# A transformer layer in fp32 on one core: transfers issued one step later, one pair of PSUM pools for all stages

## The chip, the core and the metric

The kernel runs on one core of a Trainium2 chip. Its time is the device time of one execution in microseconds (us); the medians below are of three runs. The core has five engines with in-order instruction streams: TensorE (PE; its weight loads are listed as PEld), VectorE (DVE), ScalarE (ACT), GpSimd (POOL) and SyncE (SP). SP only issues transfers here; a transfer waits in SP's queue until its buffer is free, and what is behind it in the queue waits too. ScalarE's and GpSimd's own queues carry a few more transfers. Matmul results go to PSUM, which has eight banks; each accumulator of this kernel takes a bank.

## The reference

Two token groups go through one layer: 128 context tokens and 256 latent tokens, D = 2048. Cut to what matters:

```python
def trunk_layer(x, cond, lw, attend):
    sh1, sc1, g1, sh2, sc2, g2 = modulation(cond, w_mod, b_mod)     # silu(cond) @ w_mod + b_mod
    h = rms_norm(x, n1) * (1 + sc1) + sh1
    q, k, v, u = project_in(h, w_in, q_g, k_g)                      # q, k RMS-normed per head
    attn = attend(q, k, v)                  # latent: 2-D windows with bias, plus cached context keys
    x = x + g1 * token_mixing(h, attn, u, w_na_proj, w_fnet_proj, w_gate, w_o)
    h2 = rms_norm(x, n2) * (1 + sc2) + sh2
    return x + g2 * swiglu(h2, w_gate_up, w_down), k, v
# token_mixing: (sigmoid gates * (attn @ w_na_proj, fourier(u) @ w_fnet_proj)) @ w_o
```

The outputs are both groups' tokens and the context's normed keys and values.

## The kernel before, in words

All 384 tokens go through every weight matrix together. Each operand is split into a high part (rounded, by ScalarE) and a low part (the rest, by VectorE), and a product is three matmuls (`mm3`, lines 140 to 143). **Units.** The weights come as 464 units of two 128-row tiles by 512 columns (512 KB each; some of one tile). `load_unit` (L179) puts a unit's load in SP's queue, `split_unit` (L189) makes `wh` (ACT, L137) and `wl` (DVE, L138), and `next_unit` (L202) hands PE a unit that was split two calls earlier. So a `wl` that is late by more than two units makes PE wait at the first matmul that reads it.

**Side work** is written as Python generators (`Paced`, L54) that advance by steps. A `behind` generator gets a tick in every `next_unit`, after the split; a `front` generator gets three ticks in a unit: before the split, after it, and in `mid_unit` (L198), half-way through the unit's matmuls. A rate says how many steps a tick is worth. Nothing is ordered by a planner: the order of instructions on each engine is the order in which these steps are written out. `Ahead` (L78) keeps loads a fixed number of items in front of their use; `more()` issues the next one.

**Stages**, in order of time: (1) transposes and modulated norm of x; (2) `w_in` (L619 to 647): groups of k tiles, the last group of nine tiles over eight 512-column chunks in the order 6, 7, 0 to 5; a chunk of the last group takes five units, the fifth of one tile. When a chunk is done, `after(ci)` (L589) joins `behind`: it stores the chunk and, for chunks 0 to 3 (q and k), computes the per-head norms on DVE, scales k (L610) and stores new_k. (3) `w_gate` (L984 to 998): eight passes of eight units, four accumulators each; at a pass's last unit the accumulators are copied out (`gst`, L997), the first two by DVE instead of ACT when one of the last three ticks had softmax exponentials, and stored from ACT's queue (L998). In front of it run the Fourier mixing (L660) and then the attention, eight head pairs of 15 ticks each, written in `PAIR` (L44); the modulation's rows run in front at 0.5 steps a tick. (4) `w_fnet_proj` and `w_na_proj` (L1037 to 1054), then `mixed` (L1026) gates and splits the sum; (5) `w_o` (L1142 to 1170), with x2 transposed in `behind` (`transposed`, L1123); (6) the SwiGLU feed-forward (L1266 to 1332), whose first pass also runs `inverse` (L1177) and the last `transposed`.

**Modulation rows.** `mod_rows` (L279) computes four of the six modulation vectors on DVE (L309, L311) from `w_mod` tiles `wmr`, each of which is used in two steps; per half vector there are 34 steps, the last of them a four-matmul sum (L321) and the addition of a bias row (L326).

**PSUM.** In stages 1 to 4 there are two pools of four banks, `ps` (tiles `mm`) and `pa` (tiles `at`). Most stages take accumulators from a ring, `acc_tile`: four `mm`, then three `at`, and so on without a restart (L270). The stages 5 and 6 have pools of their own over the same eight banks (L1061 to 1076): four `mm8`, three `at8` and one for the modulation rows. A pool hands out the bank that has been free longest.

Of the kernel before, what the change touches and what calls it, by code (L numbers as in the profile page):

```python
# [19 lines left out]
P = 128  # L20
# [22 lines left out]
PREP = [1.3, 1.8, 2.3, 2.3]  # L43
PAIR = "qk,b,pv,s0 m0,e0 i0,,s1 m1,e1 i1,,t0,v,,t1,,"  # L44
RATES = [1.455, 0.5, 1.1, 0.937, 0.452]
# [50 lines left out]
def trunk_kernel(ctx: ExitStack, tc: tile.TileContext, io: dict):  # L96
# [163 lines left out]
    with ExitStack() as ph:  # L260
        ps = ph.enter_context(tc.tile_pool(name="ps", bufs=4, space=PSUM))
        pa = ph.enter_context(tc.tile_pool(name="pa", bufs=4, space=PSUM))

# [5 lines left out]

        ring = itertools.cycle([mm_tile] * 4 + [at_tile] * 3)  # L270

        def acc_tile():

            return next(ring)()

        md_tile = at_tile


        def mod_rows(ty):  # L279

            def load(cc, k):
                wm = rpool.tile([P, 2, CH], F32, tag="wm", bufs=3, name=nm("wmr"))
                c0 = ty * D + cc * 2 * CH
                nc.sync.dma_start(
                    wm, w_mod[k * P : (k + 1) * P, c0 : c0 + 2 * CH].rearrange("p (i n) -> p i n", i=2)
                )
                return wm

            src = Ahead(load, [(cc, k) for cc in range(2) for k in range(KT)], 3)
            yield
            for cc in range(2):
# [8 lines left out]
                for k in range(KT):  # L302
                    _, wm = src.take()
                    for cnd in range(2):
                        if cnd:
                            yield
                        sc = csz[:, k, cnd : cnd + 1]
                        if k == 0:
                            nc.vector.tensor_scalar_mul(acc[:, cnd], wm, sc)  # L309
                        else:  # L310
                            nc.vector.scalar_tensor_tensor(  # L311
                                out=acc[:, cnd], in0=wm, scalar=sc, in1=acc[:, cnd], op0=ALU.mult, op1=ALU.add
                            )
                    src.more()
                    yield
# [105 lines left out]
        with ExitStack() as pha:  # L421
# [137 lines left out]
            def rows_and_columns():  # L559
                for ty in (2, 4, 3, 5):  # L560
                    yield from mod_rows(ty)
                    if ty in (3, 4):
                        yield
                        yield from columns(ty)
                    rows_done.add(ty)
                    yield
# [22 lines left out]
            def after(ci):  # L589
                a = acc[ci]  # L590
                if not 2 <= ci < 4:
                    nc.sync.dma_start(s_qkvu[ci], a)
# [11 lines left out]
                if ci < 2:  # L604
                    yield from inv_sqrt(rq[:, :, ci * 8 : (ci + 1) * 8], ss, HD, [P, NT, 8])
                else:
                    rk = small.tile([P, NT, 8], F32, tag="rk", name=nm("rk"))
                    yield from inv_sqrt(rk, ss, HD, [P, NT, 8])
                    a4 = a.rearrange("p t (h d) -> p t h d", d=HD)
                    nc.vector.tensor_mul(a4, a4, rk.unsqueeze(3).to_broadcast([P, NT, 8, HD]))  # L610
                    nc.sync.dma_start(s_qkvu[ci], a)
                    yield
                    nk = tmp.tile([P, 8, HD], F32, tag="junk", bufs=1, name=nm("nk"))
                    nc.vector.tensor_mul(nk, a4[:, 0], kg_row.unsqueeze(1).to_broadcast([P, 8, HD]))
                    nc.sync.dma_start(
                        new_k[:, (ci - 2) * CH : (ci - 1) * CH], nk.rearrange("p h d -> p (h d)")
                    )

            for gi, (k0, n) in enumerate(GROUPS):  # L619
                prep.due, prep.rate = DUE[gi], PREP[gi]  # L620
                if gi == len(GROUPS) - 1:
                    behind.append(Paced(expand_rpb()))
                for ci in ORDER:
                    po = [(mm_tile if gi < len(GROUPS) - 1 else acc_tile)() for _ in range(NT)]
# [35 lines left out]
        def fourier():  # L660
            with ExitStack() as st:
# [73 lines left out]
                for _ in range(6):  # L735
                    yield
                uH, uL = split_table("u", u)
                u = load_u(1)
                yield
                yield  # L740
                for pair in range(2):
                    for gi in range(2):
# [6 lines left out]
                        if pair + gi < 2:  # L749
                            uH, uL = split_table("u", u)  # L750
                            if pair == 0:
                                u = load_u(gi + 2)
# [55 lines left out]
        def attention_pair(hp, wk, values_before):  # L808
# [9 lines left out]
            def turned():  # L818
# [21 lines left out]
                nc.vector.tensor_sub(kL[:, TOK:], pk[:, TOK:], fr(kH[:, TOK:]))  # L840
                qks[0].more()

# [4 lines left out]
            def scores(qt):  # L847
# [17 lines left out]
                for j in range(2):  # L865
# [10 lines left out]
                    if qt == 0:  # L876
# [3 lines left out]
                        )  # L880
                if qt:
                    biases[0].more()

            def maxima(qt):
# [43 lines left out]
            def split_v():  # L928

                v = t["v"] = wk.tile([P, 4, 4, HD], F32R, tag="v", name=nm("v"))  # L930
                vj = vp.rearrange("p k (j d) -> p k j d", j=2)
                nc.scalar.copy(v[:, :, 0::3], vj)
                nc.vector.tensor_sub(v[:, :, 1:3], vj, fr(v[:, :, 0::3]))
                vs[0].more()

# [21 lines left out]
            def before():  # L957
                if values_before:
                    values_before()

            work = {
                "qk": turned, "b": masked, "pv": before, "v": split_v,
                **{f"{n}{j}": functools.partial(f, j) for j in range(2) for n, f in (
                    ("s", scores), ("m", maxima), ("e", exps), ("i", inverses), ("t", keys_first))},
# [19 lines left out]
        for fc8 in range(8):  # L984
            po = [mm_tile() for _ in range(4)]
            for u in range(0, KT, 2):
                wH, wL = next_unit()
                for f in range(4):
# [6 lines left out]
                    if u == KT - 2:  # L995
                        st = gst.tile([P, TOK], F32, tag="st", name=nm("gst"))
                        (nc.vector.tensor_copy if f < 2 and any(soft) else nc.scalar.copy)(st, po[f][:, :TOK])  # L997
                        nc.scalar.dma_start(s_gate[fc8][:, f], st)  # L998
        br_work.drain()
# [26 lines left out]
        def mixed(f4, gl):  # L1026
            for f in range(4):
# [3 lines left out]
                split(mixH[kt], mixL[kt], gl[0][:, f])  # L1031
                if f == 3:
                    gates.more()
                    gates.more()
                yield

        for f4 in range(4):  # L1037
            gl = [None, None]
# [21 lines left out]

    ps = ctx.enter_context(tc.tile_pool(name="ps8", bufs=4, space=PSUM))  # L1061
    pa = ctx.enter_context(tc.tile_pool(name="pa8", bufs=3, space=PSUM))
    pmd = ctx.enter_context(tc.tile_pool(name="pmd8", bufs=1, space=PSUM))

    def mm_tile():
        return ps.tile([P, CH], F32, tag="mm8", name=nm("mm"))

    def at_tile():
        return pa.tile([P, CH], F32, tag="at8", name=nm("at"))

    ring = itertools.cycle([mm_tile] * 4 + [at_tile] * 3)

    def acc_tile():
        return next(ring)()

    rows_psum["tile"] = lambda: pmd.tile([P, CH], F32, tag="md8", name=nm("md"))
    x2p = ctx.enter_context(tc.tile_pool(name="x2p", bufs=1))
# [307 lines left out]
```

## Time and profile before

| | |
|---|---|
| median of 3 runs | 2057.76 us (2057.05 to 2057.89) |
| the profiled execution | 2057.49 us, of which its span is 2055.7 us |
| PE busy in the span | 2030.5 us, 99% |
| DVE, ACT, POOL busy | 1248.7, 758.1 and 43.6 us |
| DMA engines' mean share, SP's queue | 58.8% |
| moved | 390 MB, 190 GB/s |

The profiled execution's own time is its span and 1.8 us around it. PE's busy time is the union of its matmuls, whose ends are modelled. Idle time of an engine is listed in front of the instruction that ended it, with what released it.

### The profile page before, as it was taken

To read this page: it belongs to the slowest core of one execution; us is meant where nothing else is said; L and a number is where in the kernel's file an instruction comes from. 1 tells how busy PE (TensorE), PEld (TensorE's weight loads), DVE (VectorE), ACT (ScalarE), POOL (GpSimd) and SP (SyncE) were. 2 spreads that over 40 slices of the span, in tenths; PEclk is the share of its full clock that TensorE was granted. 3 is DMA by queue.
4 is the path that set the end of the run, shared out by engine and by line. 5 is a ranking of instruction groups with operands and counts; after the bars stand their busy time and mean duration, and the time that the engine had idled before them with its cause. 6 is when DMAs were issued, how large, how long until landed. Compare 5 with 4: busy or idle time off the path is not lost.

```text
span 2055.7 us, 27509 instructions
## 1 busy us (share of the span) xinstructions
PE 2030.5 (99%) x10986; PEld 1843.7 (90%) x10986; DVE 1248.7 (61%) x1528; ACT 758.1 (37%) x1135; POOL 43.6 (2%) x92
## 2 busy tenths in 40 slices
PE   7999999999999999999999999999999999999999
PEld 5657888999999999888998999899989998999897
DVE  5634899688986787775845454544454434333456
ACT  5323232456665443334533332223322232233222
POOL 1000000000001000001000000000000000000000
PEclk9999999999999999999999999999999999999999
DMA  9887878677775775754454455544555444444453
GB/s 327 299 315 219 298 257 313 209 211 236 221 219 162 258 253 188 248 182 149 119 184 150 154 157 160 158 138 150 163 158 160 125 123 133 125 132 123 134 164 123
DMA packets 220000, 390.46 MB, mean 190 GB/s; under 512 B 28080, under 2 KB 64960, under 8 KB 219872
## 3 DMA queue, kind: packets, MB, share of 16 engines
q1 hardware_dynamic: 212704, 382.13, 58.8%
q10 hardware_dynamic: 4672, 6.31, 0.9%
q8 instruction: 86, 1.41, 0.3%
q0 software_dynamic: 2496, 0.27, 0.1%
q14 instruction: 42, 0.34, 0.1%
HBM read 371.81 MB, written 20.51 MB: 191 GB/s over the span
## 4 chain that ended last, share of the span: by engine, by line
PE 94%; DVE 2%; DMA 1%; issue 1%; SPq 1%; ACT 1%; ACTq 0%; DVEq 0%
PE mm L141 20%; PE mm L143 19%; PE mm L142 19%; PE at L143 11%; PE at L141 11%; PE at L142 11%; PE at L389 1%; DMA wm<-in_w_mod 1%; DVE accr L311 1%; PE at L856 1%; PE at L924 1%; PE at L946 1%; SPq L181 0%; SPq L365 0%; DVE wl L138 0%
## 5 line engine op out<-in xcount | busy, mean ns | idle before, releaser
L138 DVE TENSOR_TENSOR wl<-wraw,wh 128x1024 fp32r<-128x1024 f32 (+1 forms) x464 | 559.2, 1206 | 674.9 <-ACT wh L137 674.0
L137 ACT CAST wh<-wraw 128x1024 fp32r<-128x1024 f32 (+1 forms) x464 | 480.7, 1037 | 1027.9 <-PE at L142 260.3
L141 PE MATMUL mm<-hH,wh 128*128 128x384 f32 x1152 | 389.6, 338 | 1.8 <-DVE gst L997 1.2
L143 PE MATMUL mm<-hH,wl 128*128 128x384 f32 x1152 | 385.5, 335 | 0.0
L142 PE MATMUL mm<-hL,wh 128*128 128x384 f32 x1152 | 385.2, 334 | 0.0
L311 DVE SCALAR_TENSOR_TENSOR accr<-wmr,csz,accr 128x1024 f32<-128x1024 f32 x240 | 304.8, 1278 | 0.1
L141 PEld LDWEIGHTS mm<-hH,wh 128*128 128x128 f32 x1152 | 216.3, 188 | 8.3 <-issue 2.6
L142 PEld LDWEIGHTS mm<-hL,wh 128*128 128x128 f32 x1152 | 216.4, 188 | 0.0
L143 PEld LDWEIGHTS mm<-hH,wl 128*128 128x128 f32 x1152 | 216.3, 188 | 0.0
L143 PE MATMUL at<-hH,wl 128*128 128x384 f32 x640 | 213.8, 334 | 0.0
L141 PE MATMUL at<-hH,wh 128*128 128x384 f32 x640 | 213.8, 334 | 0.0
L142 PE MATMUL at<-hL,wh 128*128 128x384 f32 x640 | 213.8, 334 | 0.0
L141 PE MATMUL mm<-wh,hH 128*128 128x512 f32 x422 | 168.8, 400 | 1.8 <-DVE gl L1053 1.2
L142 PE MATMUL mm<-wl,hH 128*128 128x512 f32 x422 | 165.0, 391 | 0.9 <-DVE wl L138 0.9
L143 PE MATMUL mm<-wh,hL 128*128 128x512 f32 x422 | 164.7, 390 | 0.0
L143 PE MATMUL mm<-wh,cL 128*128 128x512 f32 x352 | 137.1, 389 | 0.0
L141 PE MATMUL mm<-wh,cH 128*128 128x512 f32 x352 | 137.0, 389 | 0.0
L142 PE MATMUL mm<-wl,cH 128*128 128x512 f32 x352 | 137.0, 389 | 0.0
L141 PEld LDWEIGHTS at<-hH,wh 128*128 128x128 f32 x640 | 120.2, 188 | 0.2
L142 PEld LDWEIGHTS at<-hL,wh 128*128 128x128 f32 x640 | 120.2, 188 | 0.2
L143 PEld LDWEIGHTS at<-hH,wl 128*128 128x128 f32 x640 | 120.2, 188 | 0.0
L141 PEld LDWEIGHTS mm<-wh,hH 128*128 128x128 f32 x422 | 79.4, 188 | 33.7 <-issue 11.9
(288 smaller groups left out, 2616.2 us busy)
## 6 DMA issues: line engine op xcount, KB each, us to landing
wraw<-in_w_gate_up SPq DMA_DIRECT2D x176, 512.0 KB, 3.7
wmr<-in_w_mod SPq DMA_DIRECT2D x128, 512.0 KB, 4.2
wraw<-in_w_down SPq DMA_DIRECT2D x88, 512.0 KB, 3.7
wm<-in_w_mod SPq DMA_DIRECT2D x64, 512.0 KB, 6.9
wraw<-in_w_gate SPq DMA_DIRECT2D x64, 512.0 KB, 5.1
wraw<-in_w_in SPq DMA_DIRECT2D x56, 512.0 KB, 6.1
wraw<-in_w_o SPq DMA_DIRECT2D x32, 512.0 KB, 5.3
wraw<-in_w_fnet_proj SPq DMA_DIRECT2D x16, 512.0 KB, 6.3
```

What stands on the lines that cost most here:

```text
L137: nc.scalar.copy(H, x)
L138: nc.vector.tensor_sub(L, x, fr(H))
L141: nc.tensor.matmul(out, aH, bH, start=start, stop=False)
L142: nc.tensor.matmul(out, aH, bL, start=False, stop=False)
L143: nc.tensor.matmul(out, aL, bH, start=False, stop=stop)
L311: nc.vector.scalar_tensor_tensor(out=acc[:, cnd], in0=wm, scalar=sc, in1=acc[:, cnd], op0=ALU.mult, op1=ALU.add)
L389: nc.tensor.matmul(pm[q : q + 32, :w], csz[:, k, :], wm[:, ty, kk + par, :], start=k < 2, stop=k >= KT - 2, tile_position=(0, q), skip_gro ...
L856: nc.tensor.matmul(po[j][:, cols], qx[rows[j], q], kx[rows[j], k], start=i == 0, stop=i == 2, tile_position=(j * HD, 0),)
L924: nc.tensor.transpose(o[:, i * P : (i + 1) * P], sc[:, j, c0 : c0 + P], ident)
L946: nc.tensor.matmul(po[j][:, CTX:TOK].rearrange("p (t q) -> p t q", t=2), w[1 + kc], x.rearrange("p (t b) q -> p t b q", t=2)[:, :, 2 * kc ...
```

## The change

It has five parts. (a) The `w_mod` row tiles of all four vectors have one `Ahead`, and the next load is issued between the two uses of a tile, when the tile before is done with, not after the second use. (b) `after` gets an empty step before its stores, and each store of a normed chunk is issued a step after the DVE instruction that makes its data. (c) In the Fourier mixing, `load_u` is issued a step after the split that frees its buffer; in the attention the three `more()` calls become ticks of their own (`lq`, `lb`, `lv`) in empty places of `PAIR`; in `mixed` the gate loads come a step later. (d) The four stores of a gate pass are issued after all four copies. (e) `ps` and `pa` live through all stages, the modulation rows take `at` tiles to the end, and the ring is three `at`, then four `mm`; it is restarted at the last `w_in` group and ahead of stage 4.

```diff
-PAIR = "qk,b,pv,s0 m0,e0 i0,,s1 m1,e1 i1,,t0,v,,t1,,"
+PAIR = "qk,b,pv,s0 m0,e0 i0,lq,s1 m1,e1 i1,,t0 lb,v,,t1,lv,"
...
-        ps = ph.enter_context(tc.tile_pool(name="ps", bufs=4, space=PSUM))
-        pa = ph.enter_context(tc.tile_pool(name="pa", bufs=4, space=PSUM))
+        ps = ctx.enter_context(tc.tile_pool(name="ps", bufs=4, space=PSUM))
+        pa = ctx.enter_context(tc.tile_pool(name="pa", bufs=4, space=PSUM))
...
-        ring = itertools.cycle([mm_tile] * 4 + [at_tile] * 3)
+        ring = None
+
+        def new_ring():
+
+            nonlocal ring
+            ring = itertools.cycle([at_tile] * 3 + [mm_tile] * 4)
...
+            return Ahead(load, [(ty, cc, k) for ty in ROWS for cc in range(2) for k in range(KT)], 3)
-            src = Ahead(load, [(cc, k) for cc in range(2) for k in range(KT)], 3)
-            yield
...
                     for cnd in range(2):
                         if cnd:
+                            if ty != ROWS[0] or cc + k:
+                                src.more()
                             yield
...
-                    src.more()
                     yield
...
             def rows_and_columns():
-                for ty in (2, 4, 3, 5):
-                    yield from mod_rows(ty)
+                src = row_weights()
+                yield
+                for ty in ROWS:
+                    yield from mod_rows(ty, src)
...
             def after(ci):
                 a = acc[ci]
+                yield
                 if not 2 <= ci < 4:
                     nc.sync.dma_start(s_qkvu[ci], a)
...
                     nc.vector.tensor_mul(a4, a4, rk.unsqueeze(3).to_broadcast([P, NT, 8, HD]))
+                    yield
                     nc.sync.dma_start(s_qkvu[ci], a)
-                    yield
                     nk = tmp.tile([P, 8, HD], F32, tag="junk", bufs=1, name=nm("nk"))
                     nc.vector.tensor_mul(nk, a4[:, 0], kg_row.unsqueeze(1).to_broadcast([P, 8, HD]))
+                    yield
                     nc.sync.dma_start(
...
                 if gi == len(GROUPS) - 1:
                     behind.append(Paced(expand_rpb()))
+                    new_ring()
...
                 uH, uL = split_table("u", u)
+                yield
                 u = load_u(1)
                 yield
-                yield
                 for pair in range(2):
...
                         if pair + gi < 2:
                             uH, uL = split_table("u", u)
+                            yield
                             if pair == 0:
                                 u = load_u(gi + 2)
                         yield
...
-                qks[0].more()
...
-                if qt:
-                    biases[0].more()
...
-                vs[0].more()
...
+                **{n: lambda of=of: of[0].more() for n, of in (("lq", qks), ("lb", biases), ("lv", vs))},
...
-                        nc.scalar.dma_start(s_gate[fc8][:, f], st)
+                        sts.append(st)
+            for f, st in enumerate(sts):
+                nc.scalar.dma_start(s_gate[fc8][:, f], st)
...
                 if f == 3:
+                    yield
                     gates.more()
                     gates.more()
                 yield
 
+        new_ring()
         for f4 in range(4):
...
-    ps = ctx.enter_context(tc.tile_pool(name="ps8", bufs=4, space=PSUM))
-    pa = ctx.enter_context(tc.tile_pool(name="pa8", bufs=3, space=PSUM))
-    pmd = ctx.enter_context(tc.tile_pool(name="pmd8", bufs=1, space=PSUM))
...
-    ring = itertools.cycle([mm_tile] * 4 + [at_tile] * 3)
...
-    rows_psum["tile"] = lambda: pmd.tile([P, CH], F32, tag="md8", name=nm("md"))
```

## Rows read from the trace of the kernel before

**Rows 1.** The page's first part: busy us of each engine, share of the span, instructions.

```profile
PE 2030.5 (99%) x10986; PEld 1843.7 (90%) x10986; DVE 1248.7 (61%) x1528; ACT 758.1 (37%) x1135; POOL 43.6 (2%) x92
```

**Rows 2.** Busy time by stretch: the stretch and its length in us, then us busy (instructions) of PE, PEld, DVE, ACT and POOL, the granted share of TensorE's clock, the DMA engines' share and GB/s.

```profile
0.00:30.00 30.00, 16.47 (x136) 12.08 (x137) 15.34 (x40) 14.75 (x36) 6.03 (x16) 0.85 0.98 295
300.00:345.00 45.00, 43.51 (x197) 36.13 (x196) 44.66 (x49) 13.16 (x14) 0.00 (x0) 1.00 0.87 302
1340.00:1700.00 360.00, 360.00 (x1956) 341.99 (x1955) 167.80 (x167) 104.53 (x118) 6.29 (x13) 1.00 0.48 145
```

**Rows 3.** What PE's matmuls waited for, over the span: us in total, times, longest us.

```profile
PE mm L141 <- DVE gl L1053: 1.2, 1, 1.2
PE mm L141 <- DVE gst L997: 1.2, 1, 1.2
...
PE mm L142 <- DVE wl L138: 0.9, 2, 0.5
PE at L143 <- DVE uL L138: 0.8, 1, 0.8
PE mm L141 <- DVE acc L645: 0.6, 1, 0.6
...
PE at L1129 <- DVE xL L1135: 0.5, 1, 0.5
```

**Rows 4.** What SP's queue waited for: the two largest lines.

```profile
SPq L181 <- DVE wl L138: 997.5, 315, 9.0
SPq L286 <- DVE accr L311: 391.8, 101, 12.0
```

**Rows 5.** DMA issues of the moved loads: out<-in, queue, count, KB each, median us from issue to landing.

```profile
wmr<-in_w_mod SPq DMA_DIRECT2D x128, 512.0 KB, 4.2
...
gl<-s_gate SPq DMA_DIRECT2D x8, 768.0 KB, 6.1
...
kp<-s_qkvu SPq DMA_DIRECT2D x8, 192.0 KB, 6.1
```

**Rows 6.** Timeline of PE at the end of `w_in`: start us, duration us, engine, line, operation, shapes, count, and in brackets the idle us ahead of it with its releaser. The first two lines are the first matmuls of the last chunk's first and second units.

```profile
318.36 0.39 PE L141 MATMUL mm<-wh,hH 128*128 128x512 f32 x1
...
322.44 0.39 PE L141 MATMUL mm<-wh,hH 128*128 128x512 f32 x1
323.37 0.50 PE L142 MATMUL mm<-wl,hH 128*128 128x512 f32 x1 [0.54 <-DVE wl L138]
```

**Rows 7.** Timelines of DVE and, last line, ACT near the end of `w_in`, same columns.

```profile
295.21 1.23 DVE L138 TENSOR_TENSOR wl<-wraw,wh 128x1024 fp32r<-128x1024 f32 x1 [1.41 <-ACT wh L137]
...
297.55 0.30 DVE L159 RECIPROCAL rss<-rss 128x24 f32<-128x24 f32 x1
...
298.53 1.76 DVE L610 TENSOR_TENSOR acc<-acc,rk 128x1536 f32<-128x1536 f32 x1
300.21 1.22 DVE L138 TENSOR_TENSOR wl<-wraw,wh 128x1024 fp32r<-128x1024 f32 x1
...
326.82 1.22 DVE L138 TENSOR_TENSOR wl<-wraw,wh 128x1024 fp32r<-128x1024 f32 x1
...
298.20 1.06 ACT L137 CAST wh<-wraw 128x1024 fp32r<-128x1024 f32 x1 [3.03 <-PE at L143]
```

**Rows 8.** Timelines of DVE and PE where the Fourier mixing waits, same columns.

```profile
382.18 0.95 DVE L138 TENSOR_TENSOR uL<-fraw,uH 128x768 fp32r<-128x768 f32 x1
...
383.19 0.39 PE L143 MATMUL at<-latH,uL 128*128 128x258 f32 x1 [0.78 <-DVE uL L138]
```

**Rows 9.** Timelines of DVE, ScalarE's queue (ACTq) and PE around the end of the seventh gate pass, same columns.

```profile
641.49 0.18 DVE L906 RECIPROCAL sm<-sm 128x4 f32<-128x4 f32 x1 [0.73 <-ACT sc L898]
641.89 0.69 DVE L326 TENSOR_TENSOR row<-row,at 128x512 f32<-128x512 f32 x1 [0.22 <-issue]
642.50 1.01 DVE L997 COPY gst<-mm 128x384 f32<-128x384 f32 x2
...
644.44 0.33 ACTq L998 DMA_DIRECT2D s_gate<-gst  x1
...
643.10 0.44 PE L141 MATMUL mm<-hH,wh 128*128 128x384 f32 x1 [1.20 <-DVE gst L997]
```

**Rows 10.** Timelines of PE and DVE in a gate unit in which a head pair's second exponentials run and no pass ends (unit 41 of 0 to 63), same columns: the last tick's transposes ahead of the next unit, and DVE's end of the unit.

```profile
563.25 1.04 PE L924 MATMUL at<-ident,sc 128*128 128x128 f32 x8
...
563.99 0.17 DVE L906 RECIPROCAL sm<-sm 128x2 f32<-128x2 f32 x1 [0.16 <-ACT sc L898]
564.07 1.26 DVE L311 SCALAR_TENSOR_TENSOR accr<-wmr,csz,accr 128x1024 f32<-128x1024 f32 x1
```

**Rows 11.** Timelines of PE, ACT and DVE at the start of `w_o`, same columns.

```profile
816.07 0.47 PE L141 MATMUL mm<-wh,hH 128*128 128x512 f32 x1 [1.21 <-DVE gl L1053]
...
822.80 1.23 DVE L138 TENSOR_TENSOR wl<-wraw,wh 128x1024 fp32r<-128x1024 f32 x1 [0.40 <-ACT wh L137]
```

**Rows 12.** Timelines of PE and ACT in the feed-forward's third unit, same columns.

```profile
962.26 0.49 PE L1188 MATMUL mm<-ident,r 128*128 128x128 f32 x3
962.80 0.52 PE L1129 MATMUL mm<-ident,x 128*128 128x128 f32 x3
...
962.28 1.05 ACT L137 CAST wh<-wraw 128x1024 fp32r<-128x1024 f32 x1 [0.91 <-PE mm L142]
963.23 0.47 ACT L1189 COPY rB<-mm 128x384 f32<-128x384 f32 x1
```

More of the change, by code (lines that the diff above doesn't have):

```diff
@@ L268, in at_tile, with row_weights, load @@
             return pa.tile([P, CH], F32, tag="at", name=nm("at"))
-        ring = itertools.cycle([mm_tile] * 4 + [at_tile] * 3)
+        ring = None
+        def new_ring():
+            nonlocal ring
+            ring = itertools.cycle([at_tile] * 3 + [mm_tile] * 4)
         def acc_tile():
             return next(ring)()
+        new_ring()
         md_tile = at_tile
-        def mod_rows(ty):
-            def load(cc, k):
+        ROWS = (2, 4, 3, 5)
+        def row_weights():
+            def load(ty, cc, k):
                 wm = rpool.tile([P, 2, CH], F32, tag="wm", bufs=3, name=nm("wmr"))
@@ L289, in load, with mod_rows @@
                 return wm
-            src = Ahead(load, [(cc, k) for cc in range(2) for k in range(KT)], 3)
-            yield
+            return Ahead(load, [(ty, cc, k) for ty in ROWS for cc in range(2) for k in range(KT)], 3)
+        def mod_rows(ty, src):
             for cc in range(2):
@@ L985, in trunk_kernel @@
             po = [mm_tile() for _ in range(4)]
+            sts = []
             for u in range(0, KT, 2):
@@ L1035, in mixed @@
                 yield
+        new_ring()
         for f4 in range(4):
@@ L1058, in trunk_kernel @@
         behind[:] = [rows]
-    ps = ctx.enter_context(tc.tile_pool(name="ps8", bufs=4, space=PSUM))
-    pa = ctx.enter_context(tc.tile_pool(name="pa8", bufs=3, space=PSUM))
-    pmd = ctx.enter_context(tc.tile_pool(name="pmd8", bufs=1, space=PSUM))
[L1065 to L1069, printed above, removed]
-    ring = itertools.cycle([mm_tile] * 4 + [at_tile] * 3)
-    def acc_tile():
-        return next(ring)()
-    rows_psum["tile"] = lambda: pmd.tile([P, CH], F32, tag="md8", name=nm("md"))
     x2p = ctx.enter_context(tc.tile_pool(name="x2p", bufs=1))
```

## The prediction

> **What bounds the kernel now.** I read the page's shares first, then the stretches, then PE's waits, then the timelines around each wait. TensorE is busy for 2030.5 of 2055.7 us [rows 1], so only 25.2 us of the span are open to any reordering. The stretches say where: 13.5 of them lie in the first 30 us, and from 1340 to 1700 us PE has none [rows 2]. The start is bound by transfers (the DMA engines are 98% busy there [rows 2]), and the change leaves its loads, their order and the matmuls alone; the transposes only take their banks in another order. I cost the start at nothing. The granted clock is 1.00 in the later stretches [rows 2], so no wait there has cost clock.
>
> What is left are single waits [rows 3]: at the end of `w_in` for two late `wl` (0.9) and for an accumulator's bank (0.6); in the Fourier mixing for `uL` (0.8); at a gate pass's end for the copy `gst` (1.2); at the start of `w_o` for a bank that `gl` still reads (1.2); and 0.5 in the x2 transposes. None of them is a wait for a weight or a stored tensor. SP's queue does wait a lot, 997.5 us for `wl` and 391.8 us for the row sums [rows 4], but the 4-deep `wraw` covers that: no line of PE's waits names `wraw`. So the first half of the change's title can move PE only through the steps that it inserts, which shift DVE's work; the second half can move it through banks. A measurement of this kernel can tell about 0.2%, 4.1 us, from no change.
>
> **The change part by part.**
>
> *Row loads.* A load now has three steps from issue to use where it had four. At 1.455 steps a unit and 4.08 us a unit (322.44 less 318.36 [rows 6]) that is 8.4 us; a tile lands in 4.2 us [rows 5]. Later stages step more slowly per us. Cost 0; without that cover DVE would stand in its queue and the next `wl` behind it. SP no longer holds the weights behind a DVE addition, worth 0 for the reason above. One loader for four vectors drops one step at each change of vector, so the second vector runs one step earlier than now and the third two.
>
> The page "DMA: Bandwidth & Descriptors" of the Trainium skill, section "Rules for kernel authors", says to issue a transfer early and wait for it late, which speaks against every such delay here. By it the sum would be larger wherever a load's cover ends; the rows show twice the landing time as cover, so I add nothing.
>
> *Other moved loads.* `lq` goes five ticks later; ten ticks, over three units and 12 us, remain before its use, against 6.1 us [rows 5]; `lb` and `lv` move by three ticks with seven and twelve left. The gate loads come half a unit later with three units left, against 6.1 us [rows 5]. Cost 0 each.
>
> *Gate stores.* Their issues used to stand between ScalarE's copies, one of them behind a DVE copy. Now four come in a row after the copies. ScalarE is 37% busy [rows 1] and casts two units ahead. Cost 0, with a rival below.
>
> *Steps in `after`.* For a k chunk the norm and scale (L159 to L610) move from the fourth unit of the next chunk to its fifth, the half unit, and the new_k product from the fifth to the next chunk's first. DVE is full here, 44.66 of 45 us [rows 2]. Now the scale of chunk 2 fills the time from 297.55 until the cast at 298.20 ends at 299.26 [rows 7]; then DVE would be idle there for 1.7 us, and the scale, 2.66 us (297.55 to 300.21), comes behind that `wl`. Today 26.6 us lie between the `wl` at 300.21 and the one at 326.82 [rows 7]. Counted from 299.3, with 2.7 more for chunk 2's scale and 0.6 less for chunk 3's new_k product, the latter starts at about 328.0 and ends at 329.2. It is read by the last chunk's third unit, which with no wait before it begins at 318.36 + 2 x 4.08 = 326.52 [rows 6], and 0.23 later reads `wl`: a wait of some 2.2 us where 0.9 stand now. Bounds are 0.9 and 2.2. I take 1.6, half-way, because the count leans on ScalarE's square root falling where I put it, and the trace does not show it there.
>
> *Banks at the end of `w_in`.* The restarted ring gives the last group's eight chunks 24 accumulators, 24 = 3 x 7 + 3, so the last chunk has three `at`, and the gate stage's four `mm` are free: the 0.6 goes. Bounds 0 and 0.6; I take all of it.
>
> *Fourier and attention ticks.* `uL` is split in the tick after the weights' split and read at the next tick, half a unit later; `uL` ends 0.8 us too late [rows 8]. With the added tick PE reads it half a unit (2 us) later still: the 0.8 goes. The branch adds three such ticks, exactly one unit, so every head pair runs one unit later against the gate passes. A pair's exponentials run in units 20 + 5p and 21 + 5p now, 21 + 5p and 22 + 5p after. Passes end with units 7, 15, ... 55, 63. Now the first exponentials meet an end at 55 (the 1.2 wait) and the second at 31. After, the first meet 31, the second meet 47, and 55 meets neither.
> At 55 the copy stands behind a reciprocal, which waits for ScalarE's exponentials, and behind the bias row's 0.69 us [rows 9]; the wait of 1.2 goes. At 31 that row is not in front of the copy, since the rows' steps are one earlier, and their four-matmul sum reaches PE ahead of the boundary: bounds 0 and 0.5; I take 0.
> At 47 a row accumulation is in front of the copy. Unit 41 shows that pattern without a boundary: reciprocal at 563.99, accumulation from 564.07, so the copy (half of 1.01 us [rows 9]) would end at 565.8, and 0.1 later PE could start; its transposes end at 564.29 [rows 10]. New wait 1.6, bounds 0.4 (no accumulation there) and 1.6. I take 1.6, since the rows step on the same ticks as before.
>
> *Start of `w_o`.* Without a restart `w_o` begins with three `mm` that stage 4 freed a set earlier, so the 1.2 goes and PE starts at 816.07 - 1.21 = 814.86 [rows 11]. DVE still has the drained `mixed` in front of the `wl` that ends at 824.03 [rows 11]; the third unit, from 814.86 + 8.17, reads it at 823.26. So 0.7 comes back; bounds 0 and 1.2.
>
> *First feed-forward pass.* Ring position 44 = 6 x 7 + 2 gives `at` and three `mm`, where now two `mm` are left. `inverse` and the last `transposed` then share one bank: the transposes at 962.80 must wait for the copy `rB`, which stands behind a cast and ends at 963.70 [rows 12]. New wait 1.0 (0.1 to restart), bounds 0 and 1.1. The x2 transposes keep their single free bank, and their 0.5.
>
> *Sum.* Gone: 0.9 + 0.6 + 0.8 + 1.2 + 1.2 = 4.7. New: 1.6 + 1.6 + 0.7 + 1.0 = 4.9. On the profiled execution's 2057.5 that makes **2057.7 us**; the median shown is 0.3 above that execution, well inside what can be told. Upper bounds of the new waits (2.2 + 0.5 + 1.6 + 1.2 + 1.1 = 6.6) give 2059.4, lower bounds (0.9 + 0 + 0.4 + 0 + 0 = 1.3) 2054.1.
>
> **The rivals.**
>
> *The waits go and nothing comes back.* Then 2057.5 - 4.7 = 2052.8. For it: five of the waits stand where a bank or a step order is changed. Against it: DVE is 99% busy in one of those places and the new order queues the same work there. The Trainium skill's page "Perfetto Trace Analysis", section "Optimizing Tensor Performance", says that independent matmul groups should rotate through different banks so that one's evacuation overlaps the next group. By that rule this rival is the outcome; the rows agree for the banks (1.8 of the 4.7), and for the rest they name late DVE work instead. Chance 0.12.
>
> *ScalarE falls behind at the gate passes.* The four stores in a row (three more issues after the last copy than now) hold the next cast, `wl` waits behind it, and PE pays at each pass. At 0.33 us an issue [rows 9] that is 1.0 us, eight times: 2057.7 + 8.0 = 2065.7. It decides only if the delay exceeds what two units' lead, 8 us, leaves over; ScalarE's share speaks against it. Chance 0.06.
>
> *The banks don't come as the ring says.* A pool hands out banks by their release, so the two bank waits (0.6 and 1.2) may stay; then the 0.7 of `w_o` and perhaps the 1.0 of the feed-forward don't come either. 2057.7 + 1.8 - 0.7 = 2058.8, or 2057.8. Chance 0.17. The forecast itself has 0.65.
>
> **How the numbers follow.** Likeliest 2057.7, its own range 2055.6 to 2059.6. The range of 8 in 10, 2054.1 to 2060.4, takes in all lower bounds and a further new wait of about a microsecond above the upper ones; it leaves out the first two rivals (0.18). Faster by over 0.2% (below 2053.65) is most of the first rival, 0.10; slower by over 0.2% (above 2061.9) is the second and a little for what I have not seen, 0.07; the rest, 0.83, is no change.
>
> **What would show it.** Right: PE's waits lose `gl`, `uL` and the `acc` line at 341 us; a wait for `gst` stands near the end of gate unit 47 (some 596 us) and none at 643; a wait of 1 us for `rB` near 963; SP's wait for the row sums shrinks from 391.8 us while the time stays. Wrong: a PE total under 2026 us, any PE wait of a kind not named here over 2 us, or casts that wait for `wraw`.

## The result and the profile after

The changed kernel takes 2062.48 us (median of 14 runs, 2060.44 to 2064.16) where the kernel before takes 2057.93 (14 runs beside it): a ratio of 1.002, 95% interval 1.0013 to 1.0027, so it is slower by some 4.5 us. The forecast was 2057.7 with a range up to 2060.4. The profiled execution took 2062.87 us, of which its span is 2061.1.

The page's shares, to be read beside [rows 1]: PE's busy time rose as well, by 2.8 us, though it computes the same.

```profile
PE 2033.3 (99%) x10986; PEld 1845.8 (90%) x10986; DVE 1248.5 (61%) x1528; ACT 758.2 (37%) x1135; POOL 44.0 (2%) x92
```

PE's waits after (us in total, times, longest), beside [rows 3]. The waits for `gl`, for `uL`, and for the accumulator at 341 us are gone, as forecast; the 1.8 for `wl` ends `w_in`, the 0.8 is `w_o`'s, and 0.6 and 0.4 are the feed-forward's. New are two waits for `gst`: 2.7 behind DVE where 1.6 was forecast, and 1.6 behind ACT, which was not foreseen.

```profile
PE mm L141 <- DVE gst L1011: 2.7, 1, 2.7
...
PE at L142 <- DVE wl L138: 1.8, 1, 1.8
PE mm L141 <- ACT gst L1011: 1.6, 1, 1.6
...
PE mm L142 <- DVE wl L138: 0.8, 1, 0.8
PE mm L1131 <- ACT rB L1191: 0.6, 1, 0.6
...
PE mm L1190 <- DVE vL L1137: 0.4, 1, 0.4
```

SP's waits after, beside [rows 4]. The first half of the change's title did what it says: SP stands 81.9 us for the row additions where it stood 391.8, and waits for the weights' own four buffers instead (`wl`, 1340.8 where it was 997.5). None of it reaches PE.

```profile
SPq L181 <- DVE wl L138: 1340.8, 405, 9.4
SPq L293 <- DVE accr L323: 81.9, 51, 4.9
```

Where the two new waits stand, in the timeline of PE after (start, length, instruction, idle time before it and what ended it): the end of gate unit 23 and the end of gate unit 47. In both the pass's last matmuls and a group of transposes are done, and the next pass's first matmul wants a bank that a copy `gst` still reads. The last line is the group of transposes that follows the second wait.

```profile
462.26 0.82 PE L937 MATMUL at<-ident,sc 128*128 128x128 f32 x6
464.63 0.45 PE L141 MATMUL mm<-hH,wh 128*128 128x384 f32 x1 [1.55 <-ACT gst L1011]
...
596.16 1.04 PE L937 MATMUL at<-ident,sc 128*128 128x128 f32 x8
599.86 0.45 PE L141 MATMUL mm<-hH,wh 128*128 128x384 f32 x1 [2.66 <-DVE gst L1011]
...
605.71 0.82 PE L937 MATMUL at<-ident,sc 128*128 128x128 f32 x6
```

Three stretches around the second wait (busy time of each engine with its instructions, then the granted clock, DMA share and GB/s). PE was busy for 1.44 of 3.4 us up to 601.30; then the clock was granted at half, 1.2 GHz instead of 2.4, for 3.4 us, and PE started 13 matmuls where it started 23 in the 3.4 us that follow. This lengthens PE's busy time by some 1.6 us, since the same matmuls take longer; the rest of the 2.8 belongs to this one execution (the second profile below has the same half clock, and PE is busy for 2030.2 us in it). In the stretches of the kernel before, such as the later ones of [rows 2], the clock is full once the start is over.

```profile
597.90:601.30 3.40, 1.44 (x8) 1.45 (x9) 2.28 (x4) 1.92 (x5) 0.00 (x0) 1.00 0.92 288
601.30:604.70 3.40, 3.40 (x13) 3.40 (x12) 2.01 (x3) 2.54 (x4) 0.00 (x0) 0.50 0.95 293
604.70:608.10 3.40, 3.40 (x23) 3.37 (x22) 3.40 (x5) 1.76 (x3) 0.00 (x0) 1.00 0.78 191
```

The account, in PE's idle time after less before: end of `w_in` 1.75 - 1.49, `uL` -0.78, unit 23 +1.55, unit 47 +2.66, the old `gst` wait at 643 us -1.20, `w_o` 0.76 - 1.21, feed-forward +0.95. That is 3.0. The 3.4 us at half speed cost 1.6 us (experiment 6), which makes 4.6, against 4.55 between the medians. Between the two profiled executions it is 5.4, since PE's first `w_in` matmul came 0.8 us later as well (30.49 against 29.68); the second profile below shows that this is no part of the change.

### The profile page after: what moved, and what is told of

Read it like the earlier page. It is cut to its first block, busy times and chain, and to the rows that moved or that the text cites. A ratio compares the mean times of both kernels' runs of the same rounds, so it can differ in the third digit from the quotient of the medians.

```text
span 2061.1 us, 27504 instructions
## 1 busy us (share of the span) xinstructions
PE 2033.3 (99%) x10986; PEld 1845.8 (90%) x10986; DVE 1248.5 (61%) x1528; ACT 758.2 (37%) x1135; POOL 44.0 (2%) x92
## 4 chain that ended last, share of the span: by engine, by line
PE 92%; DVE 3%; ACT 2%; DMA 2%; issue 1%; SPq 1%; ACTq 0%; DVEq 0%
PE mm L141 19%; PE mm L142 18%; PE mm L143 18%; PE at L142 11%; PE at L143 11%; PE at L141 11%; PE at L400 1%; DMA wm<-in_w_mod 1%; DVE accr L323 1%; DVE wl L138 1%; PE at L958 0%; PE at L872 0%; ACT wh L137 0%; PE at L937 0%; PE at L332 0%
## 5 line engine op out<-in xcount | busy, mean ns | idle before, releaser
L141 PE MATMUL mm<-hH,wh 128*128 128x384 f32 x1232 | 416.8, 338 | 4.2 <-DVE gst L1011 2.7
L143 PE MATMUL mm<-hH,wl 128*128 128x384 f32 x1232 | 412.9, 335 | 0.0
L142 PE MATMUL mm<-hL,wh 128*128 128x384 f32 x1232 | 412.6, 335 | 0.0
L141 PEld LDWEIGHTS mm<-hH,wh 128*128 128x128 f32 x1232 | 231.9, 188 | 10.4 <-issue 4.0
L142 PEld LDWEIGHTS mm<-hL,wh 128*128 128x128 f32 x1232 | 231.9, 188 | 0.0
L143 PE MATMUL at<-hH,wl 128*128 128x384 f32 x560 | 187.1, 334 | 0.0
L141 PE MATMUL at<-hH,wh 128*128 128x384 f32 x560 | 187.1, 334 | 0.0
L142 PE MATMUL at<-hL,wh 128*128 128x384 f32 x560 | 187.1, 334 | 0.0
L143 PE MATMUL mm<-wh,cL 128*128 128x512 f32 x312 | 121.6, 390 | 0.0
L142 PE MATMUL mm<-wl,cH 128*128 128x512 f32 x312 | 121.5, 389 | 0.0
```

The costliest lines, as they stand in the source:

```text
L141: nc.tensor.matmul(out, aH, bH, start=start, stop=False)
L142: nc.tensor.matmul(out, aH, bL, start=False, stop=False)
L143: nc.tensor.matmul(out, aL, bH, start=False, stop=stop)
```

## The experiments

The first theory was that the three Fourier ticks cost the time: they run every head pair one unit later against the gate passes. The rivals were the loads with their added steps, and the banks. Ratios are to the kernel before on the same chip, with 95% intervals; each variant has 11 runs.

**1. The ticks taken back out of the phase.** The changed kernel, its Fourier branch begun three ticks earlier.

```diff
-                for _ in range(6):
+                for _ in range(3):
                     yield
```

> After, with the Fourier branch begun three ticks (one unit) earlier, so that the attention stands against the gate passes as before; loads, stores, added steps and PSUM pools stay as after. Theory (the shift of one unit costs the time: the waits for gst at 464 us, 1.8, and at 600 us, 2.9, and the half clock behind the latter, 1.6): these three go, the wait of 1.2 at 643 us returns, so 2062.5 - 6.3 + 1.2 = 2057.4. Rival (loads and added steps, seen in the start's 0.95, cost the time): 2062.5 within 0.5, the gst waits merely elsewhere.

2058.7 us, ratio 1.0000 (0.9992 to 1.0009). Both new waits are gone and the clock is full. PE's waits for `gst` in this kernel come to two short ones, at 510 and 643 us:

```profile
PE mm L141 <- DVE gst L1011: 0.4, 2, 0.3
```

The phase carries the loss. The wait at 643 came back as 0.28, not as 1.2. The expected sum was 0.5 below the kernel before; the interval is 1.7 below to 1.9 above.

**2. The ticks alone**, in the kernel before.

```diff
+                yield
                 u = load_u(1)
                 yield
-                yield
...
                             uH, uL = split_table("u", u)
+                            yield
                             if pair == 0:
```

> Before, with the three Fourier ticks alone. Theory: 2057.9 - 0.9 (uL) - 1.3 (gst at 643) + 1.8 + 2.9 + 1.6 = 2062.0, with gst waits near 464 and 600 us and a stretch of half clock behind the second. Rival (loads and added steps): what the prediction said of these ticks, 2057.9 - 0.9 - 1.3 + 1.6 = 2057.3, and the clock stays at full speed.

2061.53 us, ratio 1.0016 (1.0007 to 1.0025). The total is the theory's, but not by its terms: the clock stayed full, the wait at unit 47's end is 1.58 and not 2.66, and there is one of 1.07 at the end of unit 31 (510.58). These three, less the waits that went (0.78 and 1.20), make 2.2 of the 3.3 measured; the rest is inside the interval. PE's timeline at the three pass ends:

```profile
463.42 0.45 PE L141 MATMUL mm<-hH,wh 128*128 128x384 f32 x1 [1.54 <-ACT gst L998]
...
510.58 0.45 PE L141 MATMUL mm<-hH,wh 128*128 128x384 f32 x1 [1.07 <-DVE gst L998]
...
599.15 0.45 PE L141 MATMUL mm<-hH,wh 128*128 128x384 f32 x1 [1.58 <-DVE gst L998]
```

So the forecast's 1.6 for unit 47 is what the ticks alone do, and another part of the change adds 1.1 and the half clock.

**3. The pools alone**, in the kernel before.

```diff
-        ps = ph.enter_context(tc.tile_pool(name="ps", bufs=4, space=PSUM))
+        ps = ctx.enter_context(tc.tile_pool(name="ps", bufs=4, space=PSUM))
...
+            ring = itertools.cycle([at_tile] * 3 + [mm_tile] * 4)
...
+        new_ring()
         for f4 in range(4):
...
-    ps = ctx.enter_context(tc.tile_pool(name="ps8", bufs=4, space=PSUM))
```

> Before, with the one pair of PSUM pools and the restarted rings alone. Both theories: the bank wait of 0.6 at 341 us and 1.2 at 816 us go, 0.7 for wl comes at 828, 1.0 near 966 us for vL and rB: 2057.9 - 0.1 = 2057.8. If the banks explain the slow start (transposes in another order), PE's first matmuls of w_mod columns come 0.8 us later and the time is 2058.7.

2057.65 us, ratio 0.9998 (0.9989 to 1.0007): as forecast. The 341 and 816 us waits are gone, `w_o` has 0.76 for `wl`, the feed-forward 0.38 and 0.57. The first `w_in` matmul stands at 29.59 (29.68 before), so the banks don't make the start later.

**4. The moved loads and stores alone**, with the steps in `after`, without the Fourier ticks and the pools.

```diff
+            return Ahead(load, [(ty, cc, k) for ty in ROWS for cc in range(2) for k in range(KT)], 3)
...
             def after(ci):
                 a = acc[ci]
+                yield
...
-                        nc.scalar.dma_start(s_gate[fc8][:, f], st)
+                        sts.append(st)
+            for f, st in enumerate(sts):
+                nc.scalar.dma_start(s_gate[fc8][:, f], st)
```

> Before, with all moved loads and stores and the steps added for them (row loads, after, gate stores, lq lb lv, gates), without the Fourier ticks and without the PSUM part. Theory: only the end of w_in gets longer, by 0.9: 2058.8, and 643 keeps its wait of 1.2. Rival (loads and added steps cost the time): 2061 to 2062.5, with the start 0.8 to 0.95 later and more waits for wl.

2059.99 us, ratio 1.001 (1.0001 to 1.0019), between the two expectations. PE's waits that differ from before:

```profile
PE mm L142 <- DVE wl L138: 1.8, 1, 1.8
...
PE mm L141 <- DVE acc L654: 1.2, 1, 1.2
...
PE mm L141 <- DVE gst L1003: 0.6, 1, 0.6
```

The end of `w_in` costs 1.8 where it cost 0.9, and the bank wait behind it 1.2 where it cost 0.6, since DVE is late for both; the pools take that second one away in the full change. The wait at 643, which was expected to stay at 1.2, halved. These make 0.8 of the 1.7 measured; the rest is inside the interval, and no wait shows it.

**5. The changed kernel again**, with no line of it edited, for a second profile.

> The changed kernel once more, for a second profile. If the stretch of half clock behind the wait of 2.66 us at 600 is of the kernel, it is there again near 601 to 605 and the time is 2062 to 2063; if it was of that one execution, the clock stays at full speed there and the profiled execution is some 1.6 us shorter, 2061. If the start's 0.8 was of that execution, the first w_in matmul stands between 29.6 and 30.3 us, not at 30.49.

2061.95 us, ratio 1.0021 (1.0013 to 1.003). The wait (2.72) and the half clock are there again, 596.90 to 600.30; the first `w_in` matmul stands at 29.50, before the 29.68 of the kernel before. The start varies between executions; the half clock is the kernel's. This execution took 2059.98 us, 2.9 less than the first: 1.0 of it lies before that matmul, and 1.8 between 79 and 179 us, where the same 500 matmuls took 100.20 us in the first profile and 98.43 here, both at full clock. PE's waits behind that stretch agree within 0.06 us between the two profiles. So one execution's time can't tell a microsecond here, but its waits can.

```profile
593.50:596.90 3.40, 0.84 (x8) 0.60 (x6) 3.24 (x5) 3.08 (x9) 0.00 (x0) 1.00 0.98 298
596.90:600.30 3.40, 3.25 (x10) 3.25 (x11) 1.26 (x4) 1.66 (x4) 0.00 (x0) 0.50 1.06 279
```

**6. The row addition of unit 47 half a unit later**, in the changed kernel; the later steps of the rows come one tick later with it.

```diff
+                if fc8 == 5 and u == KT - 2:
+                    rows.due -= 0.5
                 wH, wL = next_unit()
```

> After, with the bias row's addition of gate unit 47 put half a unit later, behind DVE's two gst copies. Theory (the wait at 600 us is this addition, 1.26, on top of DVE's lag): 2.66 becomes 1.4; and if the half clock hangs on that long wait, it goes too: 2062.5 - 1.3 - 1.6 = 2059.6. Rival (the exponentials' chain alone sets the copy): 2.66 stays within 0.2 and the time is 2062.5. If the clock falls whatever the wait: 2061.2.

2059.47 us, ratio 1.0009 (1.0000 to 1.0018). DVE now copies right behind the reciprocal, PE waits 1.58, and the clock stays at 2.4 GHz. Against experiment 5, on the same chip, 2.5 us are gone, 1.1 of them wait; the other 1.4 is left for the half clock. The traces give its price more closely: the next transposes start 5.85 us behind the wait's end in the first profile (605.71 less 599.86) and 4.28 behind it here (601.07 less 596.79), so 1.57.

```profile
596.12 0.17 DVE L919 RECIPROCAL sm<-sm 128x2 f32<-128x2 f32 x1 [0.16 <-ACT sc L911]
596.20 1.00 DVE L1013 COPY gst<-mm 128x384 f32<-128x384 f32 x2
...
596.79 0.44 PE L141 MATMUL mm<-hH,wh 128*128 128x384 f32 x1 [1.58 <-DVE gst L1013]
...
601.07 0.82 PE L937 MATMUL at<-ident,sc 128*128 128x128 f32 x6
```

**7. The table for the exponentials loaded earlier**, in the changed kernel.

```diff
                 values = None
+                warm = small.tile([P, 1], F32, tag="warm", bufs=1, name=nm("warm"))
+                nc.scalar.activation(out=warm, in_=ones[:, 0:1], func=AF.Exp)
                 for hp in range(8):
```

> After, with one Exp of a single column issued as the attention begins, so that ScalarE loads the table for the exponentials some 10 us before the first ones. Theory (the load of 1.28 us at 451.28 makes the first pair late): the wait for gst at 464 us falls from 1.55 to 0.3, time 2061.2, unless the wait at 600 grows by as much (2062.5). Rival (DVE's row additions make it late and the load is covered): 1.55 stays within 0.2.

2060.75 us, ratio 1.0015 (1.0007 to 1.0024), 1.2 under experiment 5. The wait at unit 23's end fell from 1.55 to 0.12; the one at 47 and its half clock stayed. In the changed kernel the load sits in front of the first pair's exponentials, and here it runs in ScalarE's idle time at 438.73. ScalarE after, then here:

```profile
451.28 1.28 ACT L911 ACT_TABLE_LOAD   x1
452.58 0.62 ACT L911 ACTIVATE sc<-sc,mx 128x384 f32<-128x384 f32 x1
```

```profile
438.73 1.28 ACT L789 ACT_TABLE_LOAD   x1
440.02 0.20 ACT L789 ACTIVATE warm<-ones 128x1 f32<-128x1 f32 x1
```

**8. Ticks and row loads**, in the kernel before: what adds 1.1 at unit 47? The theory was the rows' earlier steps. To the edit of experiment 2 it adds the change's row loads:

```diff
-                for ty in (2, 4, 3, 5):
-                    yield from mod_rows(ty)
+                src = row_weights()
+                yield
+                for ty in ROWS:
+                    yield from mod_rows(ty, src)
```

> Before, with the three Fourier ticks and the row loads' new order (one loader, one step fewer at each change of vector), and nothing else of the change. Theory (the ticks bring the pass end of gate unit 47 onto the exponentials, and the rows' earlier steps take away the wait of 1.1 at 510 us and leave DVE that much later at 600): the wait at 510 goes, the one at 599 is 2.7 where the ticks alone had 1.6, half clock follows it for 3.4 us, and the time is 2061.5 + 1.4 = 2062.9. Rival (the ticks alone set it, with the pools or other loads adding the last microsecond): 1.1 and 1.6 as with the ticks alone, full clock, 2061.5.

2059.53 us, ratio 1.0006 (0.9998 to 1.0015). Half of the theory fell. The rows' earlier step does remove the wait of unit 31, as the prediction had it, but unit 47 stays at 1.64 with full clock. Set beside each other, the two traces part at 552 us, on ScalarE. After:

```profile
551.82 0.48 ACT L1011 COPY gst<-mm 128x384 f32<-128x384 f32 x1 [0.57 <-PE mm L143]
551.88 1.85 ACTq L1014 DMA_DIRECT2D s_gate<-gst  x4
553.78 0.58 ACT L845 ACTIVATE qH<-at,qg 128x384 fp32r<-128x384 f32 x1 [1.48 <-issue]
```

With each store right behind its copy (this experiment):

```profile
551.86 0.48 ACT L1005 COPY gst<-mm 128x384 f32<-128x384 f32 x1 [0.43 <-PE mm L143]
552.37 0.38 ACTq L1006 DMA_DIRECT2D s_gate<-gst  x1
552.80 0.58 ACT L836 ACTIVATE qH<-at,qg 128x384 fp32r<-128x384 f32 x1 [0.46 <-PE at L833]
```

After the last copy four issues in a row take 1.85 us where one took 0.38, and `qH`, the first work of the next head pair, starts 0.98 later. DVE then stands idle for it where it did not here (after):

```profile
554.39 0.62 DVE L846 SCALAR_TENSOR_TENSOR qL<-at,qg,qH 128x384 fp32r<-128x384 f32 x1 [1.11 <-ACT qH L845]
```

**9. The gate stores put back behind their copies**, in the changed kernel. The theory is now that the stores make that microsecond, which DVE carries from 552 to 600 us.

```diff
-                        sts.append(st)
-            for f, st in enumerate(sts):
-                nc.scalar.dma_start(s_gate[fc8][:, f], st)
+                        nc.scalar.dma_start(s_gate[fc8][:, f], st)
```

> After, with each gate store issued again right behind its own copy. Theory (four issues in a row at the pass end of 552 us hold ScalarE's qH by 1.0, DVE waits for it, and the lag stays until the gst copies at 600): qH comes 0.4 to 0.5 behind its transposes instead of 1.5, the wait at 600 falls from 2.7 to 1.6, no half clock follows it, time 2062.0 - 1.1 - 1.4 = 2059.5. Rival (the lag comes from the moved loads or the pools): 2.7 and the half clock stay, 2062.0.

2059.19 us, ratio 1.0007 (0.9998 to 1.0016), against 1.0021 and 1.002 with the stores in a row. The intervals of this kernel and of experiment 5 still overlap, so the trace has to tell. The wait at unit 47's end is 1.56 and the clock stays full. Matmul for matmul this execution is level with the first profile just ahead of that wait and 2.67 us ahead of it from 605 us on: 1.1 of wait and 1.57 of clock. The reciprocal starts 0.3 before the transposes end.

```profile
PE mm L141 <- DVE gst L1010: 1.6, 1, 1.6
PE mm L141 <- ACT gst L1010: 1.5, 1, 1.5
```

```profile
596.17 1.04 PE L937 MATMUL at<-ident,sc 128*128 128x128 f32 x8
...
596.90 0.17 DVE L919 RECIPROCAL sm<-sm 128x2 f32<-128x2 f32 x1 [0.17 <-ACT sc L911]
```

**10. Ticks, row loads and gate stores**, in the kernel before: are these three enough? To experiment 8 it adds:

```diff
-                        nc.scalar.dma_start(s_gate[fc8][:, f], st)
+                        sts.append(st)
+            for f, st in enumerate(sts):
+                nc.scalar.dma_start(s_gate[fc8][:, f], st)
```

> Before, with the three Fourier ticks, the row loads' new order and the four gate stores in a row, and nothing else of the change. Theory (these three make the whole wait): 2.7 at 599 instead of the 1.64 without the stores, half clock for 3.4 us behind it, time 2059.5 + 1.1 + 1.4 = 2062.0. Rival (another part is needed): 1.6, full clock, 2059.5.

2061.38 us, ratio 1.0016 (1.0008 to 1.0025). They are enough, and more: the four issues took 2.44 us here, the wait is 3.2, and half clock follows it for 3.4 us.

```profile
PE mm L141 <- DVE gst L1006: 3.2, 1, 3.2
```

```profile
550.62 2.44 ACTq L1009 DMA_DIRECT2D s_gate<-gst  x4
```

**11. A version from what was found**: the changed kernel with the earlier Fourier branch, the steps in `after` undone, and the last `transposed` on the `at` banks.

```diff
-                for _ in range(6):
+                for _ in range(3):
...
                 a = acc[ci]
-                yield
...
-    behind += [Paced(inverse()), Paced(transposed(3, mm_tile), 1, 1), norm]
+    behind += [Paced(inverse()), Paced(transposed(3), 1, 1), norm]
```

> After, with the Fourier branch three ticks earlier, the added steps behind w_in's chunks undone, and the last transposed() on the at banks. Theory: the gst waits at 464 and 600 and the half clock stay away (as with the three ticks alone, 2058.7), the wait for wl at 329 falls from 1.75 to 0.9 in two, the bank wait for rB (0.6) at 966 goes and perhaps vL's 0.4: 2058.7 - 0.7 - 1.0 = 2057.0, which is 1.2 under before. Rival (waits only move on): the same sum comes back elsewhere, 2058.5.

2054.76 us, ratio 0.9989 (0.998 to 0.9998). The `rB` and `vL` waits are gone, `w_in`'s end is back to 0.9. From 160 us on PE's waits add up to 2.7 us less than before, and the medians differ by 2.7; 1.2 was expected.

**12. And `w_o`'s start**: besides, the last unit's four sums ahead of its splits.

```diff
-                nc.vector.tensor_add(gl[0][:, f], gl[0][:, f], gl[1][:, f])
+                if f4 < 3:
+                    nc.vector.tensor_add(gl[0][:, f], gl[0][:, f], gl[1][:, f])
+                elif f == 0:
+                    for g in range(4):
+                        nc.vector.tensor_add(gl[0][:, g], gl[0][:, g], gl[1][:, g])
```

> The kernel with the earlier Fourier branch, the added steps behind w_in's chunks undone and the last transposed() on the at banks, and in the last unit of the gated mixing all four sums gl + gl ahead of the four splits, so that DVE doesn't stand idle 0.6 us four times while ScalarE casts. Theory: the wl for the third unit of w_o comes some 2 us sooner, PE's 0.76 there goes: 2054.8 - 1.0 = 2053.8. Rival (DVE has other work in the queue there): 0.76 stays within 0.2, 2054.8.

2054.53 us, ratio 0.9984 (0.9975 to 0.9993): faster than both kernels. The 0.76 is gone from PE's waits; whether that adds to experiment 11 the two intervals can't tell. From 160 us on these are left:

```profile
PE at L142 <- DVE wl L138: 0.9, 2, 0.5
...
PE at L1133 <- DVE xL L1139: 0.5, 1, 0.5
PE mm L141 <- DVE gst L1009: 0.4, 2, 0.3
```

## Why the prediction was wrong

Nine of the ten terms of its sum hold, counting the 0 for unit 31. Gone as forecast: the accumulator at 341, `uL`, `gst` at 643, `gl` at 816. New as forecast: the end of `w_in` 1.75 (1.6 forecast, bounds 0.9 and 2.2; by the prediction's own figures, 329.2 less 326.75, the upper bound is 2.45), `w_o` 0.76 (0.7), the feed-forward 0.95 (1.0), unit 31 nothing (0, and for the reason given: experiments 2 and 8 differ in the row loads and in that wait). The banks came as the ring says. What failed:

- **Unit 47, mis-sized: 2.66 where 1.6 stood as the upper bound.** The step was "Unit 41 shows that pattern without a boundary". DVE's side of it held: the reciprocal comes at 597.99 and PE restarts 1.87 later, much as worked out from [rows 10]. But how far the reciprocal trails PE's transposes differs from pair to pair, and unit 41 is the most favourable of the eight: there it starts 0.3 before they end. In the kernel before, two other pairs show it 0.8 and 1.4 behind their end (a group's end is its start and length):

```profile
480.32 1.04 PE L924 MATMUL at<-ident,sc 128*128 128x128 f32 x8
482.71 0.16 DVE L906 RECIPROCAL sm<-sm 128x2 f32<-128x2 f32 x1
...
617.71 1.04 PE L924 MATMUL at<-ident,sc 128*128 128x128 f32 x8
619.53 0.17 DVE L906 RECIPROCAL sm<-sm 128x2 f32<-128x2 f32 x1 [0.17 <-ACT sc L898]
```

 With these the bounds would have been 0.4 and 3.2, and unit 51's row alone gives 2.65. After, the reciprocal trails by 0.8:

```profile
597.99 0.17 DVE L919 RECIPROCAL sm<-sm 128x2 f32<-128x2 f32 x1 [0.17 <-ACT sc L911]
598.07 1.26 DVE L323 SCALAR_TENSOR_TENSOR accr<-wmr,csz,accr 128x1024 f32<-128x1024 f32 x1
599.25 1.01 DVE L1011 COPY gst<-mm 128x384 f32<-128x384 f32 x2
```

- **Gate stores, costed at 0.** The rival of a late ScalarE had the right size, 1.0 us for three more issues, and the wrong condition. The size is partly luck: the issues took 0.46 each and not 0.33, and the first stood under the last copy. It was weighed against the weight casts, which have two units in hand. Behind the pass end at 552 us stands `qH` instead, the head of a chain that goes back and forth between ScalarE and DVE with no such lead. So it decides at one pass and not at eight, and moves the reciprocal of unit 47 from 0.3 before the transposes' end (experiment 9) to 0.8 behind it.

- **The clock, costed at 0.** "No wait there has cost clock" was true of the waits that the kernel before had; it says nothing of a longer one. Half clock for 3.4 us comes with the wait in all four profiles where it is 2.66 to 3.23 (after, experiments 5, 7, 10), and in none of the four where it is about 1.6 (experiments 2, 6, 8, 9). Its price was 1.6 by the traces of experiment 6.

- **Unit 23, not seen: 1.55.** The step "the first meet 31, the second meet 47, and 55 meets neither" asked where exponentials meet a pass end, because then DVE copies. At unit 23 ScalarE copies all four, and is late itself: the first pair's exponentials wait for a table of 1.28 us, and the chain behind them has no slack before the pass end. Before, that pass end came at a later tick of the pair. It takes both: without the shift the wait is gone (experiment 1), and without the table's load there 0.12 of it is left (experiment 7). The Trainium skill's page "ScalarE activation tables: per-element evaluation and per-set limits", section "What a function is on this engine", puts functions of different sets one load of 1283 ns apart; the row at 451.28 agrees, and what the page can't say is who waits behind it.

The claim that SP's waits don't matter held: those for the row additions fell by 310 us, and PE gained nothing. The terms that held, 0.26 + 0.95 + 0.76 less 0.78, 1.20 and 1.21, make -1.2; with unit 47 at its 1.6 that is +0.4, close to the forecast's +0.2. The error is unit 23's 1.55, the stores' 1.1 and the clock's 1.6, and the stores bring the clock's with them. The row loads' cover was thinner than said: DVE waits for `wmr`, by the row below 1.8 us in three times, all before 361 us (in the kernel before, 0.9 once), and no wait of PE stands behind it. The page "DMA: Bandwidth & Descriptors" of the Trainium skill, section "Rules for kernel authors", asks for an early issue and a late wait; the trace agrees as far as DVE.

```profile
DVE accr L323 <- DMA wmr<-in_w_mod: 1.8, 3, 1.0
```

## What to carry to other kernels

When a change shifts one stream of work against another, list every place where the two now meet and what each engine there still owes, one-off work such as a table load among it; a price from one instance is no bound, so take the spread over all instances of the pattern. A new wait may cost more than its length when the clock falls behind it. An engine that is 37% busy can still have a chain without slack: look at what stands next in its queue, not at its share.

## What the runs showed of the hardware

With a wait of PE of 2.66 to 3.23 us at the end of gate unit 47, 3.4 us were granted at 1.2 GHz, in four profiles of four; they set in between 0.15 us before the wait's end (experiment 5) and 1.4 behind it (the first profile). With 1.56 to 1.64 us there the clock stayed at 2.4 GHz, in four of four. Four transfer issues in a row on ScalarE took 1.85 and 2.44 us at the pass end of 552 us (after, experiment 10), 0.46 to 0.61 each; behind its own copy an issue took 0.33 to 0.36 us in 31 cases of 32 in the kernel before, and 0.94 in the other.
